# Norming the tokens once 1/rms is known, and emptying the projection banks on ScalarE

## Chip, core and metric

One kernel runs on one core of a Trainium2 chip. The metric is the device time of one execution in microseconds. Each comparison uses the median of several runs.

## What is computed

The kernel is one decoder layer for 512 tokens of width 1024. Cut to what matters here:

```
u    = x * rsqrt(mean(x*x) + eps) * g                 # RMSNorm of the tokens, 512 x 1024
proj = u @ w_in                                       # 1024 x 5888
qa, ka, va, qb, kb, vb, qm, gl = split(proj)          # three attentions' inputs, three gates
y0, y1, y2 = window(qa, ka, va), stick_breaking(qb, kb, vb), memory(qm, mem)
merged = sum_b sigmoid(gl_b) * (y_b @ w_branch_b)
h   = x + rms_norm(merged @ w_out)
out = h + rms_norm(swiglu_ffn(rms_norm(h)))
```

## The kernel before

**Number format.** Every large matmul is done as three: each fp32 operand is split into a high part, which ScalarE (ACT) rounds by a copy, and a low part, which VectorE (DVE) gets by a subtraction (`split`, L132 to L139). `mm3` (L164) multiplies high by high, high by low and low by high into one PSUM bank.

**Layout.** The tokens lie transposed: eight tiles of 128 features x 512 tokens (`xraw`, loaded from `xT`). `u[k]` holds the two parts of tile k. Before the change these parts are of x times the gain `g_pre`, not yet divided by the rms, because 1/rms needs the whole of x first: its squares are summed (L540 to L543, in place in `xraw`), summed over the features by a matmul with ones (`ss_x`), and turned into `rb` by `rstd_of` and `rsqrt` (L209 to L228). `rb` holds 1/rms of every token, the same in all 128 partitions. A bank of products is therefore multiplied by `rb` when it is emptied (`evac` in `proj`, L289 to L297, on DVE). For the values, whose bank has tokens on the partitions, `per_token` (L230) turns `rb` with four PE transposes into one number per token, `rs`, and `val` (L325) scales with it.

**The stream.** `Stream` holds the weight units in their order; one unit is 512 KB or less, loaded, split and multiplied. `dn.run(us)` emits so many microseconds of pieces (a piece is three to a few matmuls, by a duration written beside it); `dn.until(flag)` emits all up to a flag; loads are emitted four units and splits three units ahead. The order of the units is: four key units of the stick-breaking attention (`kb`), four query units (`qb`), six units of values in two halves (`val`, banks `pv`), then `ka`, two `qa`, the memory's keys and values, two more `qa`, and for each branch eight gate units (`g`), with four `qm` units and the branch products between. A unit of `proj` is 24 matmuls of 512 columns, `val` has 96 matmuls of 320 columns in each half.

**Banks and tiles.** Two PSUM banks (`dps`) serve `proj` (the `kb` units use four of the six `aps` banks, since they have to wait for `rb`); `val` uses four `aps` banks in each half. Nearly all tiles of 512 columns come from one pool of 68, `ck`.

**Order of the work.** The first part, to the unloading of the four `kb` banks, is in `tc.manual_schedule()`: there each engine issues in the order of the code. After it the tile framework orders each engine's instructions when the program is built, by their place in the code and by readiness; `tc.high_priority()` puts an instruction ahead of others that are ready. On the chip each engine keeps that order. After `evac`, `kb` and `qa` are split into stacked halves by `stack_parts` (L254), `qb` and `ka` by `stack_twice` (L265).

Of the kernel before, what the change touches and what calls it, by code (L numbers as in the profile page):

```python
# [13 lines left out]
AF = mybir.ActivationFunctionType  # L14
ALU = mybir.AluOpType
# [4 lines left out]
S = 512  # L20
M = 256
KC = D // P
# [81 lines left out]
def tile_kernel(ctx, tc, a):  # L104
    nc = tc.nc
# [12 lines left out]
    def ck(name, dt=F32):  # L118
        return ckp.tile([P, 512], dt, tag="ck", name=name)
# [10 lines left out]
    st = {}  # L130

    def split(raw, hi, lo):  # L132

        ins = nc.scalar.copy(hi, raw)  # L134
        lows = nc.vector.tensor_tensor(lo, raw, hi.bitcast(F32), op=ALU.subtract)  # L135
        if "behind" in st:
            after(ins, st["behind"][0])
            after(lows, st["behind"][1])
        return ins  # L139
# [22 lines left out]
    dn = Stream(w_load, w_split)  # L162

    def mm3(out, l, r, start, stop):  # L164
        (lh, ll), (rh, rl) = l, r
        nc.tensor.matmul(out, lh, rh, start=start, stop=False, skip_group_check=True)  # L166
        nc.tensor.matmul(out, lh, rl, start=False, stop=False, skip_group_check=True)  # L167
        nc.tensor.matmul(out, ll, rh, start=False, stop=stop, skip_group_check=True)  # L168
# [4 lines left out]
    def cols(hl, o, n):  # L173
        return hl[0][:, o : o + n], hl[1][:, o : o + n]
# [3 lines left out]
    def after(ins, first):  # L178
        dep = mybir.DependencyInfo(mybir.DependencyClass.NoSync, mybir.DependencyReason.DATA)
        tc.add_manual_dep(ins.ins, first.ins.name, dep, reason="order")  # L180

    def fn(*args, **kw):

        ins = nc.scalar.activation(*args, **kw)  # L184
        for p in pin:
            after(ins, p)
        since.append(ins)
        return ins
# [41 lines left out]
    def per_token(name, rb, n, bank):  # L230

        pt = bank(f"st_{name}")
        for t in range(n // P):
            nc.tensor.transpose(pt[:, t * P : (t + 1) * P], rb[:, t * P : (t + 1) * P], ident[:, :])
        rs = cst.tile([P, n // P], F32, name=f"rs_{name}")
        nc.vector.tensor_copy(rs[:, :], pt[:, :n].rearrange("p (t n) -> p t n", n=P)[:, :, 0])
        return rs
# [9 lines left out]
    u = [None] * KC  # L247

    def parts(name, t):
        h, l = ck(f"{name}h", F32R), ck(f"{name}l", F32R)  # L250
        split(t[:, :], h[:, :], l[:, :])
        return h, l

    def stack_parts(kind, idx, t):  # L254

        for e in range(2):
            r, o = 64 * e, 64 - 64 * e
            x = ck(f"{kind}s{idx}{e}", F32R)
            nc.scalar.copy(x[r : r + 64, :], t[r : r + 64, :])
            nc.vector.tensor_tensor(  # L260
                x[o : o + 64, :], t[r : r + 64, :], x[r : r + 64, :].bitcast(F32), op=ALU.subtract
            )
            st[(kind + "s", idx, e)] = x

    def stack_twice(kind, idx, t):  # L265

        for e in range(2):
            r, o = 64 * e, 64 - 64 * e
            x = ck(f"{kind}s{idx}{e}", F32R)
            lo = ck(f"{kind}l{idx}{e}", F32R)  # L270
            nc.gpsimd.memset(lo[o : o + 64, :].bitcast(F32), 0.0)
            st[(kind + "l", idx, e)] = lo
            nc.scalar.copy(x[r : r + 64, :], t[r : r + 64, :])
            nc.vector.tensor_tensor(
                lo[r : r + 64, :], t[r : r + 64, :], x[r : r + 64, :].bitcast(F32), op=ALU.subtract
            )
            nc.vector.tensor_copy(x[o : o + 64, :], t[r : r + 64, :])
            st[(kind + "s", idx, e)] = x

    def proj(kind, idx):  # L280
        def gen(hi, lo):
            ps = (aps if kind == "kb" else dps)(f"{kind}{idx}")
            for k in range(KC):
                mm3(ps[:, :], cols((hi, lo), k * P, P), u[k], k == 0, k == KC - 1)
                yield 0.65
            t = ck(f"{kind}{idx}")
            s = 0.125 if kind in ("qa", "qb") else 1.0

            def evac():  # L289
                with tc.high_priority():  # L290
                    nc.vector.scalar_tensor_tensor(t[:, :], ps[:, :], s, st["rb"][:, :], op0=ALU.mult, op1=ALU.mult)  # L291
                if kind in ("kb", "qa"):
                    stack_parts(kind, idx, t)
                elif kind in ("qb", "ka"):
                    stack_twice(kind, idx, t)
                elif kind == "qm":
                    st[("qms", idx)] = parts(f"qms{idx}", t)  # L297

            if "rb" in st:
                evac()  # L300
            else:
                st.setdefault("waiting", []).append(evac)
            st[(kind, idx)] = t

        return gen

    def gate(b, c):
        def gen(hi, lo):
            yield from proj(f"g{b}", c)(hi, lo)
            g = st[(f"g{b}", c)]  # L310

            if b in st.get("sigmoid", ()):
                dn.later(2.0, lambda: fn(g[:, :], g[:, :], AF.Sigmoid))

        return gen

# [8 lines left out]
    def val(h, q):  # L325
        def gen(hi, lo):
            if q == 0:
                st["pv"] = [aps(f"pv{h}{t}") for t in range(NT)]
            for i in range(3 if q < 2 else 2):
                k = 3 * q + i  # L330
                for t in range(NT):
                    x = (u[k][0][:, t * P : (t + 1) * P], u[k][1][:, t * P : (t + 1) * P])
                    mm3(st["pv"][t][:, :320], x, cols((hi, lo), i * 320, 320), k == 0, k == KC - 1)
                    yield 0.41
                    if k == KC - 1:
                        nc.vector.tensor_scalar(
                            v_all[:, t * 640 + h * 320 : t * 640 + (h + 1) * 320],
                            st["pv"][t][:, :320],
                            st["rs"][:, t : t + 1],
                            None,  # L340
                            op0=ALU.mult,
                        )

        return gen

    v_all = cst.tile([P, NT * 640], F32, name="v_all")
# [92 lines left out]

    for c in range(8):  # L440
        dn.add(a["w_p"][:, c].rearrange("p k n -> p (k n)"), 1024, proj("kb" if c < 4 else "qb", c % 4))
    for h in range(2):
        for q in range(3):
            n = 3 if q < 2 else 2
            dn.add(a["w_v"][:, h, 3 * q : 3 * q + n].rearrange("p k n -> p (k n)"), n * 320, val(h, q))
# [29 lines left out]
    xraw = []  # L475
# [28 lines left out]
    with tc.manual_schedule():  # L504

        idle = cst.tile([P, 512], BF16, name="idle")
        nc.vector.memset(idle[:, :], 0.0)
        pw = dps("warm")
        for i in range(WARM):
            mm(pw[:, :], idle[:, :P], idle[:, :], True, True)  # L510

        first_load(nc.scalar, 0)
        first_table = nc.scalar.preload_act_table_set("natural_log_exp_and_others")
        g_pre = const("g_pre", [P, KC])
        load_x(0, 3)
        first_load(nc.sync, 1)
        load_x(3, 5)
        first_load(nc.sync, 2)
        load_x(5, 8)
        dn.loaded = dn.have = FIRST  # L520
        first_split(0, 0)
        gain_split(0)
        for i in range(1, FIRST):
            first_split(i, 0)
        gain_split(1)
        gain_split(2)
        for p in (1, 2):
            for i in range(FIRST):
                first_split(i, p)
            for k in range(*PIECE[p]):  # L530
                if u[k] is None:
                    gain_split(k)
        dn.ahead(4, 3)
        gens = [dn.units[i]["mm"](his[i], los[i]) for i in range(FIRST)]
        for k in range(KC + 1):
            for g in gens:
                next(g, None)
        dn.at = FIRST
        xacc = ck("xacc")
        nc.scalar.activation(xacc[:, :], xraw[0][:, :], AF.Square)  # L540
        for k in range(1, KC):
            nc.scalar.activation(xraw[k][:, :], xraw[k][:, :], AF.Square)
            nc.vector.tensor_tensor(xacc[:, :], xacc[:, :], xraw[k][:, :], op=ALU.add)  # L543
        while dn.at < 4:
            dn.piece()
        st["rb"] = rstd_of("x", xacc, S, aps)
        for f in st.pop("waiting"):
            f()
# [16 lines left out]
    none_r = cst.tile([P, P], F32R, name="none_r")  # L565
    nc.gpsimd.tensor_copy(none_r[:, :], none[:, :])

    st["rs"] = per_token("x", st["rb"], S, aps)
    dn.until("sb_ready")


# [519 lines left out]
    rb = {}  # L1091
# [317 lines left out]
```

## Time and profile before

| what | value |
|---|---|
| median of three runs | 813.15 us (813.1 to 813.63) |
| profiled execution | 813.76 us, span 812.0 us |
| TensorE (PE) busy | 800.4 us, 99% of the span, 4727 matmuls |
| DVE busy | 589.7 us, 73% |
| ACT busy | 440.0 us, 54% |
| POOL busy | 85.0 us, 10% |
| share of PE in the chain that ended last | 92% |

Engines: PE multiplies, PEld loads its weights beside it, DVE is VectorE, ACT is ScalarE, POOL is GpSimd, SP issues most DMAs. A row of the timeline has the start in us, the duration in us, the engine, the line of the kernel, the operation, output<-inputs, the shapes and the count; in brackets stands the idle time before it and what ended it. A matmul's duration is longer than the distance to the next one, since matmuls overlap; the distance is what PE needs for one. A row of waits has who waited for whom, the total in us, how many times and the longest.

### The profile page before, as it was taken

The numbers are of one execution on the slowest core, as the hardware profiler recorded it, in microseconds if no ns is written. First come the engines' busy times: TensorE is split into PE (matmuls) and PEld (weight loads), VectorE is DVE, ScalarE is ACT, GpSimd is POOL, SyncE is SP. The second block draws the span as 40 slices with busy tenths as digits, with TensorE's granted clock in tenths as the row PEclk, the third lists the DMA queues.
The fourth block names the chain that finished last, engine by engine and source line by source line (L and its number), as shares of the span: only waits on it lengthen the run. The fifth ranks groups of instructions, "written<-read, shape, count | busy, mean of one in ns | idle before, by whom it ended". The sixth has DMA issues, their size and how long they took to land.

```text
span 812.0 us, 12349 instructions
## 1 busy us (share of the span) xinstructions
PE 800.4 (99%) x4727; PEld 702.8 (87%) x4727; DVE 589.7 (73%) x939; ACT 440.0 (54%) x787; POOL 85.0 (10%) x103
## 2 busy tenths in 40 slices
PE   9999999999999999999999999999999999999996
PEld 6789888778888888888888899999999999988885
DVE  5886779656488843773384869977676777898797
ACT  6554667556655533552362566655555555666573
POOL 3003200000000000221004200110000000205200
PEclk9999999999999999999999999999999999999998
DMA  8334534321221223213359936887767662759902
GB/s 270 121 113 142 184 103 132 93 61 53 78 79 52 79 82 99 79 52 100 86 163 377 246 66 167 248 209 186 194 177 191 176 172 88 177 131 224 207 1 104
DMA packets 37741, 112.94 MB, mean 139 GB/s; under 512 B 4625, under 2 KB 6177, under 8 KB 37681
## 3 DMA queue, kind: packets, MB, share of 16 engines
q1 hardware_dynamic: 29232, 86.07, 33.2%
q0 software_dynamic: 8016, 25.68, 16.5%
q8 instruction: 37, 0.61, 0.3%
q10 hardware_dynamic: 432, 0.39, 0.2%
q14 instruction: 24, 0.19, 0.1%
HBM read 108.46 MB, written 3.67 MB: 138 GB/s over the span
## 4 chain that ended last, share of the span: by engine, by line
PE 92%; DVE 3%; DMA 2%; ACT 1%; issue 1%; SPq 0%; ACTq 0%; DVEq 0%
PE g L166 5%; PE g L167 5%; PE g L168 5%; PE gx L166 5%; PE gx L168 5%; PE gx L167 5%; PE z L171 4%; PE br L166 3%; PE br L167 3%; PE br L168 3%; PE gy L168 3%; PE gy L166 3%; PE gy L167 3%; PE x L168 2%; PE x L167 2%; PE x L166 2%
## 5 line engine op out<-in xcount | busy, mean ns | idle before, releaser
L134 ACT CAST hi<-raw 128x1024 fp32r<-128x1024 f32 (+2 forms) x64 | 65.8, 1035 | 109.7 <-issue 51.8
L134 ACT CAST hi<-gw 128x1024 fp32r<-128x1024 f32 x77 | 79.8, 1048 | 82.3 <-DVE gw L994 40.1
L135 DVE TENSOR_TENSOR lo<-gw,hi 128x1024 fp32r<-128x1024 f32 x77 | 93.5, 1223 | 33.6 <-ACT hi L134 33.6
L135 DVE TENSOR_TENSOR lo<-raw,hi 128x1024 fp32r<-128x1024 f32 (+2 forms) x64 | 78.2, 1226 | 17.6 <-ACT hi L134 17.5
L166 PE MATMUL g<-uh,hi 128*128 128x512 f32 x192 | 75.6, 394 | 0.0
L168 PE MATMUL g<-uh,lo 128*128 128x512 f32 x192 | 74.8, 389 | 0.0
L167 PE MATMUL g<-ul,hi 128*128 128x512 f32 x192 | 74.8, 389 | 0.0
L291 DVE SCALAR_TENSOR_TENSOR g<-g,rb_x 128x512 f32<-128x512 f32 x24 | 16.4, 689 | 54.7 <-PE g L168 54.5
L976 POOL DMA_DIRECT2D gw<-in_w_gu x27 | 23.4, 906 | 187.4 <-DMA gw<-in_w_gu 61.2
L168 PEld LDWEIGHTS g<-uh,lo 128*128 128x128 f32 x192 | 36.0, 188 | 7.6
L166 PEld LDWEIGHTS g<-uh,hi 128*128 128x128 f32 x192 | 36.1, 188 | 7.5 <-issue 0.3
L167 PEld LDWEIGHTS g<-ul,hi 128*128 128x128 f32 x192 | 36.1, 188 | 7.1
L134 ACT CAST hi<-r 128x1024 fp32r<-128x1024 f32 (+1 forms) x24 | 23.6, 982 | 19.9 <-PE y L168 5.3
L167 PE MATMUL x<-lo,lh 128*128 128x512 f32 x88 | 34.2, 389 | 0.0
L166 PE MATMUL x<-hi,lh 128*128 128x512 f32 x88 | 34.2, 389 | 0.0
L168 PE MATMUL x<-hi,ll 128*128 128x512 f32 x88 | 34.1, 389 | 0.0
L135 DVE TENSOR_TENSOR lo<-r,hi 128x1024 fp32r<-128x1024 f32 (+1 forms) x24 | 27.1, 1131 | 3.7 <-ACT hi L134 3.6
L184 ACT ACTIVATE e<-e 128x384 f32<-128x384 f32 (+1 forms) x48 | 26.9, 561 | 1.5
L134 ACT CAST hi<-bp 128x512 fp32r<-128x512 f32 x33 | 19.1, 620 | 13.4 <-PE y L168 4.8
L641 DVE SCALAR_TENSOR_TENSOR e<-z,e 128x384 f32<-128x384 f32 (+1 forms) x24 | 14.3, 598 | 15.9 <-ACT e L184 15.9
L166 PE MATMUL gx<-T4h,hi 128*128 128x256 f32 x88 | 25.1, 285 | 0.4 <-ACT hi L134 0.4
L166 PE MATMUL gy<-N22h,hi 128*128 128x256 f32 x88 | 25.1, 285 | 0.2 <-ACT hi L134 0.2
(539 smaller groups left out, 2614.0 us busy)
## 6 DMA issues: line engine op xcount, KB each, us to landing
gw<-in_w_gu SPq DMA_DIRECT2D x57, 512.0 KB, 4.9
raw<-in_w_p SPq DMA_DIRECT2D x38, 512.0 KB, 3.5
gw<-in_w_gu POOLq DMA_DIRECT2D x27, 512.0 KB, 7.7
raw<-in_w_br SPq DMA_DIRECT2D x12, 512.0 KB, 3.6
bp<-in_w_dn SPq DMA_DIRECT2D x22, 256.0 KB, 8.1
r<-in_w_dn POOLq DMA_DIRECT2D x10, 512.0 KB, 8.2
raw<-in_w_out SPq DMA_DIRECT2D x8, 512.0 KB, 3.6
bp<-in_w_dn POOLq DMA_DIRECT2D x11, 256.0 KB, 12.6
```

Source lines behind the costliest of these rows:

```text
L134: ins = nc.scalar.copy(hi, raw)
L135: lows = nc.vector.tensor_tensor(lo, raw, hi.bitcast(F32), op=ALU.subtract)
L166: nc.tensor.matmul(out, lh, rh, start=start, stop=False, skip_group_check=True)
L167: nc.tensor.matmul(out, lh, rl, start=False, stop=False, skip_group_check=True)
L168: nc.tensor.matmul(out, ll, rh, start=False, stop=stop, skip_group_check=True)
L171: return nc.tensor.matmul(out, l, r, start=start, stop=stop, skip_group_check=True)
L184: ins = nc.scalar.activation(*args, **kw)
L291: nc.vector.scalar_tensor_tensor(t[:, :], ps[:, :], s, st["rb"][:, :], op0=ALU.mult, op1=ALU.mult)
L641: nc.vector.scalar_tensor_tensor(x, z[i][:, :n], 0.0, x, op0=ALU.max, op1=ALU.add)
L976: nc.gpsimd.dma_start(gw[(n, key)][:, :], g_src(n, i, j), accum_op=ALU.add)
```

## The change

The tokens are normed once `rb` is there: `normed(k)` multiplies `xraw[k]` in place by the gain and `rb` on DVE and splits it anew (ACT copy, DVE subtraction) into two tiles. After each of the eight, 2.5 us of the stream are emitted. After the `qb` units (flag `plain`) `u` holds the new parts, and `st["whole"]` is set. All units from the values on read these. Their banks need no scale: `proj` empties them by an ACT multiplication with a constant, or, for a gate whose branch's sigmoids have already been applied, by the sigmoid itself, which `gate` applied later before. `val` empties its banks by plain copies at high priority, even tiles on ACT and odd ones on DVE. `per_token` is no longer called for x. The squares go to tiles of their own, since `xraw` is still needed.

```diff
+            whole = "whole" in st
             def evac():
                 with tc.high_priority():
-                    nc.vector.scalar_tensor_tensor(t[:, :], ps[:, :], s, st["rb"][:, :], op0=ALU.mult, op1=ALU.mult)
+                    if not whole:
+                        nc.vector.scalar_tensor_tensor(t[:, :], ps[:, :], s, st["rb"][:, :], op0=ALU.mult, op1=ALU.mult)
+                    elif kind[0] == "g" and int(kind[1]) in st.get("sigmoid", ()):
+                        fn(t[:, :], ps[:, :], AF.Sigmoid)
+                    else:
+                        nc.scalar.mul(t[:, :], ps[:, :], s)
...
     def gate(b, c):
         def gen(hi, lo):
             yield from proj(f"g{b}", c)(hi, lo)
-            g = st[(f"g{b}", c)]
-            if b in st.get("sigmoid", ()):
-                dn.later(2.0, lambda: fn(g[:, :], g[:, :], AF.Sigmoid))
...
                     if k == KC - 1:
-                        nc.vector.tensor_scalar(
-                            v_all[:, t * 640 + h * 320 : t * 640 + (h + 1) * 320],
-                            st["pv"][t][:, :320],
-                            st["rs"][:, t : t + 1],
-                            None,
-                            op0=ALU.mult,
-                        )
+                        with tc.high_priority():
+                            vt = v_all[:, t * 640 + h * 320 : t * 640 + (h + 1) * 320]
+                            if t % 2 == 0:
+                                nc.scalar.copy(vt, st["pv"][t][:, :320])
+                            else:
+                                nc.vector.tensor_copy(vt, st["pv"][t][:, :320])
...
         dn.add(a["w_p"][:, c].rearrange("p k n -> p (k n)"), 1024, proj("kb" if c < 4 else "qb", c % 4))
+    dn.mark("plain")
...
-            nc.scalar.activation(xraw[k][:, :], xraw[k][:, :], AF.Square)
-            nc.vector.tensor_tensor(xacc[:, :], xacc[:, :], xraw[k][:, :], op=ALU.add)
+            xs = ck(f"xs{k}")
+            nc.scalar.activation(xs[:, :], xraw[k][:, :], AF.Square)
+            nc.vector.tensor_tensor(xacc[:, :], xacc[:, :], xs[:, :], op=ALU.add)
...
-    st["rs"] = per_token("x", st["rb"], S, aps)
+    def normed(k):
+        x = xraw[k]
+        nc.vector.scalar_tensor_tensor(
+            x[:, :], x[:, :], g_pre[:, k : k + 1], st["rb"][:, :], op0=ALU.mult, op1=ALU.mult
+        )
+        return tuple(t[:, :] for t in parts(f"n{k}", x))
+
+    un = []
+    for k in range(KC):
+        un.append(normed(k))
+        dn.run(2.5)
+    dn.until("plain")
+    u[:] = un
+    st["whole"] = True
     dn.until("sb_ready")
```

## The prediction

> **What bounds the kernel now.** I read the page's shares and chain first, then who made TensorE (PE) wait, then the order of PE's and VectorE's (DVE's) instructions around the places where it waited, then busy time by stage.
>
> ```profile
> span 812.0 us, 12349 instructions
> PE 800.4 (99%) x4727; PEld 702.8 (87%) x4727; DVE 589.7 (73%) x939; ACT 440.0 (54%) x787; POOL 85.0 (10%) x103
> PEclk9999999999999999999999999999999999999998
> PE 92%; DVE 3%; DMA 2%; ACT 1%; issue 1%; SPq 0%; ACTq 0%; DVEq 0%
> ```
> ```profile
> PE warm L171 <- DVE idle L507: 1.3, 1, 1.3
> PE st_x L234 <- DVE rb_x L216: 0.9, 1, 0.9
> PE pv L166 <- DVE v_all L336: 0.9, 1, 0.9
> PE gx L166 <- ACT hi L134: 0.4, 1, 0.4
> PE qb L166 <- DVE qb L291: 0.4, 1, 0.4
> ...
> ```
>
> PE is busy for 800.4 of 812.0 us and is 92% of the chain that ended last. So work taken from DVE or given to ScalarE (ACT) is worth nothing by itself; it counts only where PE waits. The list of PE's waits (total, times, longest; three more are 0.3 or less) is short. The change can touch three of them: `st_x`, `qb` and `pv`. The next view is PE's order around these three.
>
> ```profile
> 32.86 0.39 PE L167 MATMUL qb<-ul,hi 128*128 128x512 f32 x1
> 33.09 0.39 PE L168 MATMUL qb<-uh,lo 128*128 128x512 f32 x1
> 34.42 0.66 PE L234 MATMUL st_x<-c_ident,rb_x 128*128 128x128 f32 x4 [0.94 <-DVE rb_x L216]
> 34.83 0.47 PE L166 MATMUL qb<-uh,hi 128*128 128x512 f32 x1
> ...
> 41.76 0.30 PE L166 MATMUL pv<-hi,uh 128*128 128x320 f32 x1
> ...
> 44.83 0.31 PE L166 MATMUL pv<-hi,uh 128*128 128x320 f32 x1
> 45.55 0.50 PE L166 MATMUL qb<-uh,hi 128*128 128x512 f32 x1 [0.41 <-DVE qb L291]
> ...
> 69.34 0.41 PE L166 MATMUL pv<-hi,uh 128*128 128x320 f32 x1 [0.87 <-DVE v_all L336]
> ```
>
> Matmuls of 512 columns start 0.23 us apart (32.86, 33.09), those of 320 columns 0.147 (22 of them from 41.76 to 44.83). Three losses are seen. From 33.32 to 34.83, 1.51 us, PE waits for 1/rms and transposes it. From 44.98 to 45.55, 0.57 us, the third query unit (qb2) waits for a bank. At 69.34 the value matmuls wait 0.87 us. Together they are 2.95 us, and this is all that the change can win. One more thing counts: between 41.76 and 44.98 PE had no bank for qb2 and did 22 value matmuls (3.2 us) instead. DVE, in the same stretch, shows why the bank was late:
>
> ```profile
> 33.67 0.69 DVE L216 SCALAR_TENSOR_TENSOR rb_x<-t_x,rb_x 128x512 f32<-128x512 f32 x1
> 34.40 0.69 DVE L291 SCALAR_TENSOR_TENSOR kb<-kb,rb_x 128x512 f32<-128x512 f32 x1
> 35.77 1.39 DVE L260 TENSOR_TENSOR kbs<-kb,kbs 64x512 fp32r<-64x512 f32 x2 [0.50 <-ACT kbs L259]
> ...
> 37.78 1.15 DVE L135 TENSOR_TENSOR lo<-raw,hi 128x960 fp32r<-128x960 f32 x1
> ...
> 41.74 1.39 DVE L260 TENSOR_TENSOR kbs<-kb,kbs 64x512 fp32r<-64x512 f32 x2 [0.69 <-ACT kbs L259]
> 43.14 0.69 DVE L291 SCALAR_TENSOR_TENSOR kb<-kb,rb_x 128x512 f32<-128x512 f32 x1
> 43.75 1.15 DVE L135 TENSOR_TENSOR lo<-raw,hi 128x960 fp32r<-128x960 f32 x1
> 44.81 0.68 DVE L291 SCALAR_TENSOR_TENSOR qb<-qb,rb_x 128x512 f32<-128x512 f32 x1
> ```
>
> The bank of qb0 was full soon after 36 (six matmuls after 34.83), but DVE emptied it at 44.81, behind all four key units (kb0 to kb3: 0.69 to unload, 1.39 to split). It did so although it idled for 0.69 before 41.74 and ran two weight splits in gaps. So the unload of qb0 does not slip into the key chain, high priority or not. My reading, not shown, is that its tile gets a slot of the shared pool only after those of earlier instructions.
>
> ```profile
> 34.40:45.50 11.10, 10.72 (x56) 9.25 (x56) 9.77 (x14) 6.96 (x10) 0.00 (x0) 1.00 0.16 44
> 45.50:56.60 11.10, 11.05 (x49) 9.14 (x50) 10.01 (x17) 4.50 (x8) 0.00 (x0) 1.00 0.36 101
> 56.60:69.30 12.70, 11.87 (x81) 11.60 (x79) 11.31 (x18) 9.31 (x17) 3.75 (x4) 1.00 0.54 173
> ```
>
> Columns after the stretch's length: PE, PEld, DVE, ACT. From 34.4 to 69.3 DVE is busy 31.1 of 34.9 us: 3.8 us are free, just where the change adds work.
>
> **The change part by part.** Prices of the added work:
>
> ```profile
> L291 DVE SCALAR_TENSOR_TENSOR g<-g,rb_x x24: 677/692/692, 172.6 to 407.9; 128x512 f32<-128x512 f32 x24
> L184 ACT ACTIVATE g<-g x24: 612/624/630, 208.7 to 409.2; 128x512 f32<-128x512 f32 x24
> L134 ACT CAST mgh<-g x8: 612/621/624, 412.7 to 431.6; 128x512 fp32r<-128x512 f32 x8
> L135 DVE TENSOR_TENSOR mgl<-g,mgh x8: 681/684/687, 414.4 to 433.9; 128x512 fp32r<-128x512 f32 x8
> L336 DVE TENSOR_SCALAR v_all<-pv,rs_x x8: 536/541/546, 68.7 to 82.9; 128x320 f32<-128x320 f32 x8
> ```
>
> (1) Norming: eight times a DVE scale (0.69), an ACT copy (0.62) and a DVE subtraction (0.68). That is 11.0 us on DVE and 5.0 on ACT, where DVE has 3.8 us free.
>
> (2) The four transposes and the copy to `rs_x` go: PE runs on from 33.32 instead of 34.83, a gain of 1.51.
>
> (3) The squares go to tiles of their own: same instructions, nothing. No DMA and no POOL instruction is added or moved on its queue. The shared pool of 68 tiles holds, while both sets of token parts live, 16 old, 16 new, at most 8 raw, 8 key parts, 16 query parts and 4 unsplit queries; each normed tile frees its raw one, so it stays below 68, with little to spare. A shortage would hold the last norming until the queries are done: case E.
>
> (4) ACT unloads all 33 later banks (24 gates, 1 ka, 4 qa, 4 qm) at about 0.62 instead of DVE at 0.69; the late gates of the last branch need one ACT instruction where there was a DVE and an ACT one. PE waits nowhere in those stages and one unit's 24 matmuls take 5.5 us for an unload of 0.62, so zero; if ACT's queue is in the way for longer than the other bank's unit lasts, that excess is paid. I keep 0 to 2 us for it.
>
> (5) Value banks: four of eight unloads go to ACT, all at high priority. The wait of 0.87 goes, since one unload (0.54) is shorter than the two tiles that PE still has banks for (six matmuls, 0.9 us).
>
> (6) The value units now read the normed tokens. So they cannot stand in while qb2 waits: the stand-in of 41.76 to 44.98 is gone unless the first normed token tile is ready.
>
> The stall follows. PE ends qb1 at 41.76 - 1.51 = 40.2. DVE has 1/rms at 34.36. The key chain is 4 x 0.69 + 4 x 1.39 = 8.3 us. Its four gaps, where it waits for ACT, now hold ready work: three scales (2.1) and a weight split (1.15). With the unload of qb0 (0.69) this ends at 34.36 + 8.3 + 3.2 + 0.7 = 46.6. If the subtractions of the first three tiles come first (the code's order, if slots are given in that order), it ends at 48.7, but then the first normed tile is there at about 46.6 and value matmuls stand in from then. Both ways PE idles from 40.2 to 46.6, 6.4 us. From below: with gaps unfilled and free, 43.4, a stall of 3.2; from above: 48.7 without a stand-in, 8.5. I take 6.4, which both orders give. Later, PE has 11 us of queries and 14 us of first-half values (96 x 0.147), to 71.7; DVE still has, after 46.6, three unloads (2.1), four query stacks (8.9, each two 0.69 and two 0.42 beside row L274/L277), the rest of the norming (8.9) and two splits (2): 21.9 us, to 68.5, so it is just in time.
>
> ```profile
> L274 DVE TENSOR_TENSOR qbl<-qb,qbs x8: 674/686/689, 47.5 to 59.1; 64x512 fp32r<-64x512 f32 x8
> L277 DVE CAST qbs<-qb x8: 421/422/424, 48.2 to 57.9; 64x512 fp32r<-64x512 f32 x8
> ```
>
> Stall 6.4 less the three losses 2.95: +3.45 us.
>
> (7) A second price of the stall is PE's speed after it. The program's start shows it:
>
> ```profile
> 1.35 4.43 PE L171 MATMUL warm<-idle 128*128 128x512 bf16 x11 [1.35 <-DVE idle L507]
> 1.75 0.15 PEld L171 LDWEIGHTS <-idle 128*128 128x128 bf16 x1 [0.28 <-issue]
> 2.18 0.15 PEld L171 LDWEIGHTS <-idle 128*128 128x128 bf16 x1 [0.28 <-issue]
> ```
>
> After the idle start, 512-column matmuls come 0.43 us apart, against 0.23 later, though the clock row reads full. Eleven of them lose 11 x 0.20 = 2.2 us. No later idle in this trace is over 1.3 us, so it does not tell whether 6.4 us brings the slow rate back. From below 0, from above 2.2, a whole new start. I take 2.2, since the only long idle that the trace has was followed by it.
>
> The Trainium skill, "TensorE: Matmul & The Clock Gate", section "HAM oscillation", says that PE idle for more than about 3.4 us falls back to half clock, for about 3.4 us of work. By that rule the term would be 1.7, an estimate, and the time 818.3; the start above (4.4 us at half rate) fits it, and no stall here tests it.
>
> Sum: the profiled execution took 813.76 us (its span is 812.0), 0.6 above the median of 813.15. It gains 2.95 and loses 6.4 and 2.2: 819.4, or **818.8** on the median.
>
> **Rivals.**
> B, the stall comes but PE keeps its rate: +3.45, 816.6. For it: nothing in the trace slows after the short waits. Against: they are short.
>
> C, a short stall: DVE's gaps stay unfilled and the unload ends at 43.4 to 44.5; stall 3.2 to 4.3, +0.3 to +1.4, so 813.4 to 814.6. Against it: two splits were put into such gaps before.
>
> D, faster: DVE unloads qb0 before PE ends qb1 at 40.2, in the gap at 35.1 or 37.8. Then PE never stops for qb2; queries end at 51.2, the last normed tile is due 12.3 us later at 63.5, and DVE's work to there, with three stacks ahead of it, is 32 us from 34.36, to 66.3; with the stacks after it, 59.7. So between -2.95 and 0; at -1.5 it is 811.6. Against it: the same gaps passed qb0 by in this trace. It decides at 40.2.
>
> E, worse: the stall as forecast, and norming also late for the value units, or ACT late with later banks: +2 to +4 more, 821 to 823.
>
> That the relief of DVE pays nothing after 83 us is in all of them.
>
> **How the numbers follow.** This kernel's three runs spread 0.07%; 0.2% (1.6 us) is about what can be told. Chances: forecast 0.38, B 0.22, C 0.16, D 0.15, E 0.09. The forecast, B and E are slower (0.69), C is the same but for its upper edge (0.15 and 0.01), D is faster about four times in five (0.12 and 0.03). Slower 0.70, same 0.18, faster 0.12. The range 812.6 to 822 leaves out D and part of E; the forecast's own range is 817 to 820.5.
>
> **What would show it.** In the changed profile: no `st_x`; the wait of PE for `qb` grows from 0.4 to over 5 us and ends on DVE L291's successor or a normed tile; DVE nearly without idle from 34 to 69; `pv` no longer waits near 69; after the stall, PE's matmuls 0.43 apart for some us; PE's waits after 83 us as short as now. The prediction is wrong if DVE unloads qb0 before 40.2, if the queries' order is another, or if PE finds other ready work in the stall.

## The result: 8.8 us slower, and the profile after

| | before | after |
|---|---|---|
| median of the compared runs | 813.36 us (813.1 to 813.63) | 822.19 us (821.67 to 822.56) |
| ratio after to before | | 1.0102, interval [1.009, 1.0114] |
| profiled execution / span | 813.76 / 812.0 us | 821.67 / 819.5 us |

The forecast was 818.8, slower with a chance of 0.70. The direction held. The time lay above the forecast's own range (817 to 820.5) and just above the upper end of the whole range (822.0); the ratio, applied to the 813.15 that the forecast started from, gives 821.4.

The page of the changed kernel: span, busy time, and the clock row in 40 slices of 20.5 us.

```profile
span 819.5 us, 12347 instructions
PE 801.7 (98%) x4723; PEld 704.1 (86%) x4723; DVE 575.9 (70%) x917; ACT 459.2 (56%) x824; POOL 84.9 (10%) x103
PEclk9989999999999999999999999999999999999998
```

DVE lost 14 us of work and ACT gained 19; PE's own work hardly changed. Who made PE wait (total, times, longest):

```profile
PE pv L166 <- ACT n0h L134: 7.6, 1, 7.6
...
PE pv L166 <- DVE v_all L344: 0.7, 1, 0.7
...
PE pv L166 <- ACT v_all L342: 0.4, 1, 0.4
```

There is one new wait of 7.6 us, for the high part of the first normed tile. `st_x` and `qb` are gone from the list, and `v_all` waits twice instead of once. PE's order around these places:

```profile
39.54 0.39 PE L168 MATMUL qb<-uh,lo 128*128 128x512 f32 x1
47.48 0.64 PE L166 MATMUL pv<-hi,n0h 128*128 128x320 f32 x1 [7.56 <-ACT n0h L134]
...
50.54 0.43 PE L167 MATMUL pv<-lo,n0h 128*128 128x320 f32 x1
50.80 0.31 PE L168 MATMUL pv<-hi,n0l 128*128 128x320 f32 x1
...
52.12 0.39 PE L166 MATMUL qb<-uh,hi 128*128 128x512 f32 x1
...
75.57 0.41 PE L166 MATMUL pv<-hi,n0h 128*128 128x320 f32 x1 [0.36 <-ACT v_all L342]
76.97 0.41 PE L166 MATMUL pv<-hi,n0h 128*128 128x320 f32 x1 [0.70 <-DVE v_all L344]
```

The last matmul of qb1 starts at 39.54 and takes its 0.23 us, so PE stands from 39.77 to 47.48, 7.71 us. From 47.48 to 50.80 it does 11 value matmuls in 3.32 us; at 0.147 each they would need 1.62, so 1.70 us are lost to the slow rate. Then the spacing is 0.147 again, and qb2 starts at 52.12. DVE and ACT show why so late:

```profile
33.27 0.69 DVE L216 SCALAR_TENSOR_TENSOR rb_x<-t_x,rb_x 128x512 f32<-128x512 f32 x1
...
34.60 1.41 DVE L575 SCALAR_TENSOR_TENSOR xT<-xT,c_g_pre,rb_x 128x512 f32<-128x512 f32 x2
38.08 0.74 DVE L575 SCALAR_TENSOR_TENSOR xT<-xT,c_g_pre,rb_x 128x512 f32<-128x512 f32 x1
38.74 1.15 DVE L135 TENSOR_TENSOR lo<-raw,hi 128x960 fp32r<-128x960 f32 x1
...
41.93 1.40 DVE L575 SCALAR_TENSOR_TENSOR xT<-xT,c_g_pre,rb_x 128x512 f32<-128x512 f32 x2
...
45.41 1.15 DVE L135 TENSOR_TENSOR lo<-raw,hi 128x960 fp32r<-128x960 f32 x1
...
48.03 0.69 DVE L135 TENSOR_TENSOR n0l<-xT,n0h 128x512 fp32r<-128x512 f32 x1
48.64 0.75 DVE L575 SCALAR_TENSOR_TENSOR xT<-xT,c_g_pre,rb_x 128x512 f32<-128x512 f32 x1
...
50.56 0.68 DVE L135 TENSOR_TENSOR n2l<-xT,n2h 128x512 fp32r<-128x512 f32 x1
51.17 0.68 DVE L294 SCALAR_TENSOR_TENSOR qb<-qb,rb_x 128x512 f32<-128x512 f32 x1
```
```profile
45.53 1.26 ACT L259 CAST kbs<-kb 64x512 fp32r<-64x512 f32 x2 [2.22 <-DVE kb L294]
46.81 0.62 ACT L134 CAST n0h<-xT 128x512 fp32r<-128x512 f32 x1
```

The first normed tile was scaled at 34.60, but ACT copies it only at 46.81, right behind the copies of the last key unit, although ACT had idled for 2.22 us before those. That copy ends at 47.43 and lets PE go on. DVE unloads the bank of qb0 at 51.17, behind the whole key chain (to 48.0, with five scales and two weight splits in its gaps), three low parts and two more scales. The windows of both stretches (length, PE, PEld, DVE, ACT, POOL, granted clock, DMA share, GB/s):

```profile
34.40:45.50 11.10, 5.53 (x25) 4.25 (x23) 10.85 (x17) 5.71 (x8) 1.04 (x2) 0.93 0.16 45
45.50:56.60 11.10, 9.12 (x40) 8.10 (x41) 10.94 (x17) 5.28 (x9) 0.00 (x0) 0.76 0.15 44
```

DVE is full (10.85 and 10.94 of 11.1), PE is not, and the second stretch's clock is 0.76.

**A ruler for the rest.** Between profiled executions `rb` comes at 32.77 to 34.35 us whatever the kernel, so whole spans compare badly. Two stretches are steadier: from the start of `rb` (33.67 before, 33.27 after) to `pbias`, the first matmul behind the values, and from `pbias` to the last matmul. Their rows in the kernel before and in the changed one:

```profile
82.75 0.91 PE L171 MATMUL pbias<-oh,rb 32*128 32x384 f32 x2
804.68 0.39 PE L168 MATMUL x<-hi,ll 128*128 128x512 f32 x1
```
```profile
89.93 0.91 PE L171 MATMUL pbias<-oh,rb 32*128 32x384 f32 x2
812.12 0.39 PE L168 MATMUL x<-hi,ll 128*128 128x512 f32 x1
```

Worked out so for all profiles, with the compared ratios:

| kernel | rb to pbias | pbias to last matmul | ratio to before, interval |
|---|---|---|---|
| before | 49.08 | 721.93 | 1 |
| after | 56.66 | 722.19 | 1.0102 [1.009, 1.0114] |
| after_again (the changed kernel once more) | 56.67 | 722.23 | 1.0106 [1.0092, 1.0119] |
| a_queries_first | 61.60 | 722.20 | 1.0136 [1.0118, 1.0154] |
| a_fill | 56.45 | 722.21 | 1.0091 [1.0078, 1.0105] |
| a_dve_unload | 56.66 | 721.95 | 1.0088 [1.0074, 1.0102] |
| a_own | 49.61 | 722.22 | 1.0014 [1.0005, 1.0023] |
| a_own_act | 48.16 | 723.70 | 0.9999 [0.999, 1.0008] |
| b_norm_unused | 50.98 | 721.97 | 1.0022 [1.0013, 1.0031] |
| b_own | 47.97 | 721.93 | 0.9988 [0.998, 0.9996] |
| b_own_late | 49.54 | 721.94 | 0.9999 [0.999, 1.0009] |
| b_own_late_pri | 48.04 | 721.94 | 0.9999 [0.999, 1.0008] |
| b_best | 47.91 | 721.94 | 0.9993 [0.9984, 1.0002] |

The change costs 7.58 us before `pbias` and 0.26 behind it, 7.84 together. The rows of PE in this profile add up to nearly the same: 7.71 of standing, 1.70 of slow rate, 1.06 of new waits for `v_all` and 0.26 at the back, less the 2.95 that went away, are 7.78. What remains to the 8.8 of the medians are the scatter of the start and 0.41 outside the span (821.67 - 819.5 = 2.17, before 1.76), whose cause isn't settled.

### The profile page after: what moved, and what is told of

The parts are those of the page before. It is cut to its first block, busy times and chain, and to the rows that moved or that the text cites. A ratio compares the mean times of both kernels' runs of the same rounds, so it can differ in the third digit from the quotient of the medians.

```text
span 819.5 us, 12347 instructions
## 1 busy us (share of the span) xinstructions
PE 801.7 (98%) x4723; PEld 704.1 (86%) x4723; DVE 575.9 (70%) x917; ACT 459.2 (56%) x824; POOL 84.9 (10%) x103
## 4 chain that ended last, share of the span: by engine, by line
PE 93%; DVE 5%; ACT 1%; issue 1%; DVEq 0%; ACTq 0%
PE g L166 5%; PE g L168 5%; PE g L167 5%; PE gx L166 5%; PE gx L168 5%; PE gx L167 5%; PE z L171 4%; PE br L166 3%; PE br L168 3%; PE br L167 3%; PE gy L168 3%; PE gy L166 3%; PE gy L167 3%; PE x L168 2%; PE x L167 2%; PE x L166 2%
## 5 line engine op out<-in xcount | busy, mean ns | idle before, releaser
L134 ACT CAST hi<-gw 128x1024 fp32r<-128x1024 f32 x77 | 79.8, 1048 | 82.3 <-DVE gw L1012 40.2
L135 DVE TENSOR_TENSOR lo<-bp,hi 128x512 fp32r<-128x512 f32 x33 | 22.3, 708 | 5.8 <-ACT hi L134 5.5
L166 PE MATMUL gx<-B11h,hi 128*128 128x256 f32 x88 | 25.1, 285 | 0.2 <-ACT B11h L923 0.2
L166 PE MATMUL mx<-woh,mgh 128*128 128x512 f32 x64 | 25.0, 391 | 0.0
L168 PE MATMUL gw<-B21h,lo 128*128 128x256 f32 x88 | 25.0, 284 | 0.0
L168 PE MATMUL gy<-N22h,lo 128*128 128x256 f32 x88 | 25.0, 284 | 0.0
L167 PE MATMUL gx<-B11l,hi 128*128 128x256 f32 x88 | 25.0, 284 | 0.0
L168 PE MATMUL mx<-woh,mgl 128*128 128x512 f32 x64 | 24.9, 389 | 0.0
```

## The experiments

Kernels a_ start from the changed kernel, b_ from the kernel before. The theory: the stall is made by the order in which slots of the shared pool are given (the raw tile of qb0 stands behind earlier code), together with the loss of the stand-in. The rivals: the half rate after the stall, ACT's later unloads, or DVE's overload as such.

**a_fill: keep PE warm through the stall.** 32 matmuls of zeros that nobody reads, behind qb1.

```diff
+        if k == 4:
+            pf = aps("fill")
+            for i in range(32):
+                ins = mm(pf[:, :], idle[:, :P], idle[:, :], True, True)
+                after(ins, st["last_qb1"])
```

> The changed kernel with 32 extra matmuls of zeros (512 columns, 0.23 us each, 7.3 us in all) on TensorE right behind the second query unit, where it idles from 39.77 to 47.48 us. Their results are not used; nothing else is changed. Theory (the stall costs twice, the idle itself and a slow restart): the idle is now filled, the value matmuls after it are 0.147 us apart instead of 0.27, and the time falls by the slow restart alone, 12 matmuls x 0.125 us = 1.5 to 1.7 us, to 820.5. Rival (the 0.27 us spacing has another cause, such as waiting for the normed parts): no change, 822.2.

Measured: 821.59 us, between the theory's 820.5 and the rival's 822.2. PE's waits and the window:

```profile
PE pv L166 <- DVE v_all L346: 0.9, 1, 0.9
PE pv L168 <- DVE n0l L135: 0.7, 1, 0.7
PE qb L166 <- DVE qb L296: 0.5, 1, 0.5
...
```
```profile
45.50:56.60 11.10, 9.54 (x47) 7.14 (x46) 10.94 (x17) 5.29 (x9) 0.00 (x0) 1.00 0.16 46
```

The clock is back from 0.76 to 1.00, so the slow rate came from the stall. But the time hardly moved: PE, faster now, waits 0.7 for a low part and 0.5 for the bank of qb0, both from DVE, and 0.3 for the first normed tile. From `rb` to `pbias` it saves 0.21 us of the 1.70 lost in the rows. The slow restart ran beside DVE's late unload.

**a_dve_unload: the later banks emptied by DVE again**, unscaled. (The gates whose bank is emptied by the sigmoid kept that on ACT, other than the expectation says.)

```diff
-                        nc.scalar.mul(t[:, :], ps[:, :], s)
+                        nc.vector.tensor_scalar(t[:, :], ps[:, :], s, None, op0=ALU.mult)
```

> The changed kernel with the 33 later projection banks emptied by VectorE again, by a multiplication with a constant, and the sigmoids of the last branch's late gates fused no longer but left out there (so those gates stay without their sigmoid; the time is what is asked). The value banks stay as changed. Theory (nothing after 83 us waits for these unloads): 822.2 within 0.5 us. Rival (ScalarE's queue delays banks in the later stages and part of the 8.8 us is lost there): faster by 1 us or more.

Measured: 821.25 us, below the expected 821.7 to 822.7. Its two rows:

```profile
89.97 0.91 PE L171 MATMUL pbias<-oh,rb 32*128 32x384 f32 x2
811.92 0.39 PE L168 MATMUL x<-hi,ll 128*128 128x512 f32 x1
```

The back part takes 721.95 us, as before the change; with ACT it takes 722.19. All five profiles with ACT's unloading and no slow stretch there have 722.19 to 722.23, the seven without it 721.93 to 721.97. So the 0.26 behind `pbias` is ACT's unloading; of the 33 banks 25 went back to DVE here. The front keeps its loss. By the medians the gain is larger, 0.94 us; 0.38 of it lies outside the span (2.17 in the changed kernel, 821.09 - 819.3 = 1.79 here), and a_own, with ACT's unloading, has 1.76 there, so this part isn't explained by it.

**a_own: tiles of their own for the four unscaled queries**, instead of slots of the shared pool.

```diff
+    qown = [cst.tile([P, 512], F32, name=f"qown{i}") for i in range(4)]
...
-            t = ck(f"{kind}{idx}")
+            t = qown[idx] if kind == "qb" else ck(f"{kind}{idx}")
```

> The changed kernel with four tiles of their own for the unscaled queries qb, instead of slots of the shared pool; the work is the same. Theory (the unload of qb0 is held until earlier instructions have their slots, so TensorE finds no bank): VectorE unloads qb0 in the first gap, about 35.5 us, TensorE runs through all four query units to about 50.7, the idle of 7.7 us and the slow restart go, and what is left is up to 2 us where the last normed tile is late: 811 to 814. Rival (VectorE simply has 11 us too much work in this stretch, in whatever order): TensorE waits as long, but for the normed tiles, after the queries: 819 or more.

Measured: 815.06 us (814.22 to 815.97), above the expected 811 to 814. DVE's unload of qb0, and PE's waits that are left:

```profile
35.92 0.69 DVE L296 SCALAR_TENSOR_TENSOR qown<-qb,rb_x 128x512 f32<-128x512 f32 x1
```
```profile
PE pv L169 <- DVE lo L137: 1.6, 1, 1.6
...
PE pv L170 <- DVE n7l L137: 0.5, 1, 0.5
...
PE pv L170 <- DVE n5l L137: 0.4, 1, 0.4
```

No instruction changed, only where a tile lives: the unload moved from 51.17 to 35.92, the stall went, and rb to `pbias` fell by 7.05 us. So the shared pool's slot is what held the unload and made the stall. That the slots are given in the code's order is the reading; that the pool of 68 was short of free ones would have the same cure, and a_queries_first below speaks for the order. The norming still overloads DVE: three waits of 2.5 us together stand where the 2.95 were won.

**b_norm_unused: the kernel before, with the eight normings added and nobody reading them.**

```diff
+    for k in range(KC):
+        normed(k)
+        dn.run(2.5)
+    dn.until("plain")
```

> The kernel before with the eight normings added at the same place (and the squares in tiles of their own), but with nobody reading them: values, gates and all else read the old parts and scale as before. Theory (the norming's 11 us on VectorE hurt only because the value matmuls can no longer stand in while the third query unit has no bank): qb0 is unloaded at about 51 as in the changed kernel, but value matmuls fill the time; 813.4 to 815. Rival (the load on VectorE alone makes it slow): 819 or more.

Measured: 815.58 us, just above the expected 813.4 to 815 and far from the rival's 819. DVE's unload and PE's waits:

```profile
50.92 0.69 DVE L291 SCALAR_TENSOR_TENSOR qb<-qb,rb_x 128x512 f32<-128x512 f32 x1
```
```profile
PE pv L166 <- DVE v_all L336: 1.3, 1, 1.3
PE pv L167 <- DVE lo L135: 1.2, 2, 0.9
```

The unload is as late as in the changed kernel (50.92 against 51.17), yet the price up to `pbias` is 1.90 us in place of 7.58: values that read the old parts stand in. A late bank alone makes no stall; a late bank without other work for PE does.

**after_again and a_queries_first.** The changed kernel once more, beside a version whose normings are emitted behind the queries:

```diff
-    un = []
-    for k in range(KC):
-        un.append(normed(k))
-        dn.run(2.5)
     dn.until("plain")
-    u[:] = un
+    u[:] = [normed(k) for k in range(KC)]
```

> The changed kernel itself, as the measure for the filled and the reordered kernels on one chip. Expected 822.2 within 0.5 us if the clock's slow restart costs what the filled kernel seemed to save (0.6 us against the other call); 821.5 if that was a difference between calls only.

> The changed kernel with all eight normings emitted behind the four query units instead of between their pieces; same instructions. Theory (slots of the pool are given in the code's order): the unload of qb0 then waits for the key chain alone and comes at about 47.5 us instead of 51.2, but the normed tiles come only behind the query stacks, at about 63, so TensorE idles twice, 7.7 us before the third query unit and 3 us before the values: 823 to 825. Rival (the normings between the pieces are what delays TensorE, and queries first is the remedy): 816 to 818.

Measured: after_again 822.24 us, 1.0106 [1.0092, 1.0119], so by the medians a_fill and a_dve_unload gain 0.65 and 0.99 us over it. Its profile is a second one of the same program, and the slow restart is longer in it: PE stands for 8.26 us, then does 16 matmuls at the slow rate (48.23 to 52.89) and loses 2.3 us by it in place of 1.70, and waits for `v_all` only once, 0.70. Yet `rb` to `pbias` takes 56.67 us, against 56.66. So PE's losses in this stretch stand in for one another, and the sum of PE's rows above is one way of booking them.

a_queries_first 824.16 us (823.1 to 827.15), 1.0136 [1.0118, 1.0154], as forecast; the waits in its profile (of its longest execution):

```profile
PE qb L166 <- ACT kbs L259: 7.6, 1, 7.6
PE pv L166 <- ACT n0h L134: 2.7, 1, 2.7
```

DVE unloads qb0 from 47.37 to 48.05, 12.4 us behind the end of `rb` in place of 17.2, with the order of the code alone changed. (The first row names ACT's last key copy, which ends at 48.09.) The first stall is as long as before, though no low part of a normed tile stands ahead of qb0's unload any more: the query comes sooner, but now no values stand in at all. A second stall of 2.7 follows for the norming. Moving the normings in the code trades one wait for another; it doesn't take the unload out of the key chain.

**a_own_act: a_own, with the queries' cross-half copies (L277) on ACT**, to relieve DVE.

```diff
-            nc.vector.tensor_copy(x[o : o + 64, :], t[r : r + 64, :])
+            nc.scalar.copy(x[o : o + 64, :], t[r : r + 64, :])
```

> The changed kernel with own tiles for the unscaled queries, and the eight (later also two) copies across halves in the query and key split moved from VectorE (0.42 us each) to ScalarE. Theory (with the order mended, only VectorE's 11 us too much are left, seen as three waits of TensorE of 0.4, 0.5 and 1.6 us): VectorE loses 3.4 us of work ahead of these waits, they shrink to under 0.7 us together, and the time is 1 to 2.5 us below that of the kernel with own tiles alone, 0.9970 to 0.9995 of before. Rival (ScalarE's queue becomes the one that is late): no gain against own tiles alone, 1.001 or more of before.

Measured: 813.75 us (812.47 to 815.07). That is 1.3 below a_own, within the 1 to 2.5 expected; the ratio, 0.9999, is just above its expected range. The front part is 1.45 us shorter than a_own's. But in this profile (the slowest execution, 815.07) the back part is 1.5 longer:

```profile
82.25 0.91 PE L173 MATMUL pbias<-oh,rb 32*128 32x384 f32 x2 [1.14 <-POOL rb L601]
...
85.48 0.63 PE L169 MATMUL ka<-n0l,hi 128*128 128x512 f32 x1
85.91 0.63 PE L170 MATMUL ka<-n0h,lo 128*128 128x512 f32 x1
```

Behind a wait of 1.14 us the matmuls come 0.43 apart until about 87.9. In the kernel before, no slow rate was seen behind waits of 0.9 us.

**b_best, b_own, b_own_late, b_own_late_pri: what the other parts are worth without norming.** b_own is the kernel before with the own tiles of a_own. b_own_late also emits the transposes of 1/rms behind the queries:

```diff
+    dn.until("plain")
     st["rs"] = per_token("x", st["rb"], S, aps)
```

b_own_late_pri also empties the value banks at high priority (DVE); b_best does that with the even ones on ACT.

> The kernel before, without norming, with three edits that take its three losses of 2.95 us one by one: own tiles for the unscaled queries (0.57), the transposes of 1/rms emitted behind the query units (the wait of 1.1; the transposes' 0.41 stays), and the value banks emptied at high priority, even ones by ScalarE with the per-token scale (0.87). Theory (these waits are all that the change could win): 2.0 to 2.5 us faster than before, 0.9970 to 0.9978. Rival (TensorE waits elsewhere instead, as VectorE is as full as ever): within 0.5 us of before.

> The kernel before with tiles of their own for the four unscaled queries, and nothing else changed. The theory (the pool's slots are given in the order of the code, so that qb0's unload stands behind the key chain): qb0 is unloaded near 36 to 38 us instead of 44.81, PE no longer waits for qb (0.41 and the 0.16 around it go), and the value matmuls no longer have to stand in; the transposes (1.5) and the wait for v_all (0.9) stay. So 0.3 to 0.7 us faster than before, ratio 0.9990 to 0.9997, hardly to be told from it; and the changed kernel with such tiles (1.0014) is then 1.2 to 1.8 us slower than this one, which is the price of the change itself. Rival (the unload's place comes from DVE's load, not from the slots): qb0 is unloaded after 42 us and nothing changes.

> The kernel before with own tiles for the four unscaled queries, and the four transposes of 1/rms emitted behind the queries. Theory: PE runs from qb0 through the queries without waiting for 1/rms, 1.2 us (the wait of 0.94 and the queue around it; the four transposes still cost about 0.3) and the 0.57 at qb2 go; the wait for v_all near 69 stays. 1.3 to 2.0 us faster than before, ratio 0.9975 to 0.9984. Rival: PE, early by that much, waits the same time at the next late buffer (a weight part or v_all), and the ratio is 0.9992 to 1.0000, as it was with the values' banks shared with ACT.

> As the run before this (own tiles, late transposes), and the values' banks emptied at high priority, all eight by DVE. Theory: of the waits of PE for v_all (0.9 before, 1.5 where ACT emptied half of these banks) 0.5 or less is left, since DVE does not have to wait for ACT's queue; 0.4 to 0.9 us faster than the run before this, ratio to the kernel before 0.9965 to 0.9978. Rival: the wait for v_all moves or grows, since DVE is busy with the queries' halves there, and it equals the run before this within 0.4 us.

Measured: b_own 812.29 us (811.83 to 815.48), b_best 812.68 (811.87 to 815.57), b_own_late_pri 813.12 (812.29 to 814.92), b_own_late 813.88 (812.04 to 815.33). Only b_own's interval stays below 1. In b_own, DVE's unload of qb0, PE's waits and its `pbias`:

```profile
36.88 0.68 DVE L293 SCALAR_TENSOR_TENSOR qown<-qb,rb_x 128x512 f32<-128x512 f32 x1
```
```profile
PE pv L168 <- DVE v_all L338: 0.5, 1, 0.5
...
PE st_x L236 <- DVE rb_x L218: 0.2, 1, 0.2
```

The unload moved from 44.81 to 36.88 and the wait for `qb` is gone, as the theory had it; the interval of the size (1.0 us, 0.3 to 1.6) takes in what was expected (0.3 to 0.7). The late transposes then give nothing that can be told: PE waits for `v_all` instead, 1.5 us in b_best (even banks on ACT), 1.6 in b_own_late_pri, 2.3 in b_own_late. None of the three reached its theory, and by the ratios their rivals hold (b_best's 0.6 us is just over the 0.5 named). In b_own_late a slow stretch follows that wait:

```profile
68.95 0.41 PE L168 MATMUL pv<-hi,uh 128*128 128x320 f32 x1 [2.29 <-DVE v_all L338]
...
70.95 0.47 PE L170 MATMUL pv<-hi,ul 128*128 128x320 f32 x1
71.22 0.47 PE L168 MATMUL pv<-hi,uh 128*128 128x320 f32 x1
```

So the fastest version that I found, though not told apart from b_best, is the kernel before with four tiles of its own for the unscaled queries. With the same tiles the change itself costs 2 to 3 us: by the ratios 1.0014 against 0.9988, by the medians 815.06 against 812.29, by the two stretches 1.64 + 0.29.

## Why the prediction was right in kind and short in size

Right, with its rows or runs:

- The place and the mechanism. PE stopped behind qb1, for a normed tile, because qb0's bank was emptied behind the key chain and the values could no longer stand in. The reading on slots, "not shown" then, is shown by a_own and b_own (one edit of where a tile lives moved the unload by 15 us in the one and, counted from `rb`, by 7 in the other; a_queries_first supports the order), and the lost stand-in by b_norm_unused.
- Term (2): no `st_x`, no wait for 1/rms. Term (3): no loss is seen from the squares' own tiles.
- Term (4): put at zero, it is 0.26 us behind `pbias` (a_dve_unload).
- Norming just in time for the first half of the values: the list of PE's waits of the changed kernel has none for `n1` to `n7`. It was in time because the stall had delayed PE; without the stall (a_own) PE waits for `n5l` and `n7l`.

Wrong:

- **The stall, 6.4.** It was 7.71. Counted from the end of `rb`, PE stopped at 5.81 us (the prediction: 5.84) and restarted at 13.52 (12.24). The step that failed is the filling of the key chain's gaps: "three scales (2.1) and a weight split (1.15)" were five scales and two splits. That put the last key unit's unload on DVE at 44.80, and ACT's copy of the first normed tile, which ends the stall, behind the copies of that unit at 45.53. Then two more scales stood between the low parts, so qb0 was unloaded at 51.17, not at 48.0. Whether tiles of their own for the normed parts would let ACT copy the first one in its earlier gaps was not tried.
- **Term (7), 2.2 for a slow restart.** The restart was slow, and its rows lose 1.70. But taking it away (a_fill) gives back 0.21 between `rb` and `pbias`, and 0.6 by the medians, since DVE unloads qb0 only at 51.17 and PE would have waited there instead. The term took a loss in PE's rows for a price without asking what ends next.
- **Term (5), a wait of 0.87 gone.** It became 0.36 + 0.70 = 1.06 (0.70 in after_again's profile). High priority did not bring DVE's unload ahead of the two parts of the memory (`ml`) that it did first:

```profile
74.85 1.66 DVE L242 SCALAR_TENSOR_TENSOR ml<-mT,c_g_mem,mh 128x256 fp32r<-128x256 f32 x2 [0.37 <-ACT mh L241]
76.44 0.88 DVE L344 COPY v_all<-pv 128x320 f32<-128x320 f32 x2
```

In the prediction's own sum, 6.4 + 2.2 - 2.95 = 5.65, the rows put 7.71 for 6.4 (+1.31), 1.70 for 2.2 (-0.50), 1.06 of new `v_all` waits (+1.06) and 0.26 for the later banks (+0.26): 7.78. The slow rate's 1.70 counts there as a loss of PE's rows; with PE at full rate (a_fill) most of it came back as waits for DVE.

Of the rivals, C (a short stall, gaps unfilled) and D (qb0 emptied before 40.2) fell with the row at 51.17. D's order is what a_own forces (unload at 35.92), and there D's own doubt was borne out: the last normed tiles came late, and instead of 811.6 it took 815.06. B was, in effect, near the truth on the slow rate: PE lost the rate but the kernel hardly paid. E named the right total (821 to 823) for another reason.

## What to carry to other kernels

When a list of waits shows an engine emptying a bank late although it idled before, look for what its output tile waits for: in these runs a slot of the shared pool came by the order of the code, and a tile of its own can move the instruction by many microseconds, for the space of the tile. Before you move work ahead of a critical chain, look for the work that stands in while the chain is late; if the change makes that work depend on the chain, the hidden delay becomes a stall. And price a slow stretch only after asking which other engine sets the next deadline.

## What the hardware showed that I had not expected

- PE's half rate comes in stretches of a fixed length. Narrow windows of the granted clock show it at 0.50 from 43.96 to 50.78 in the changed kernel (6.83 us), 42.63 to 52.87 in after_again (10.24), 45.29 to 52.12 in a_dve_unload (6.83), 43.57 to 53.81 and 64.05 to 70.88 in a_queries_first (10.24 and 6.83), 70.33 to 73.74 in b_own_late and 84.46 to 87.88 in a_own_act (3.41 each): one, two or three times 3.41 us. Three rows, all within such stretches, in the changed kernel, after_again and b_own_late:

```profile
44.00:50.70 6.70, 3.22 (x11) 2.96 (x12) 6.54 (x11) 2.90 (x5) 0.52 (x1) 0.50 0.24 73
42.70:52.80 10.10, 4.57 (x16) 4.31 (x17) 9.91 (x16) 4.30 (x8) 0.52 (x1) 0.50 0.24 80
70.40:73.70 3.30, 3.30 (x14) 3.30 (x14) 1.00 (x1) 0.00 (x0) 0.00 (x0) 0.50 0.63 194
```

- In these seven the clock falls 2.2 to 5.4 us after PE has stopped, whether PE has resumed or not. Behind the stalls of 7.6 to 8.3 us, and behind 2.9 us of standing in a_queries_first, the slow rate is there when PE resumes; behind the waits of 2.29 (b_own_late) and 1.14 us (a_own_act) it comes 1.4 and 2.2 us later. Waits of 1.6 (a_own, b_own_late_pri) and 1.5 us (b_best) show none in their profiles. The Trainium skill, "TensorE: Matmul & The Clock Gate", section "HAM oscillation", has half clock after more than about 3.4 us of idle: the stalls of 7.6 to 8.3 us agree; the 2.9, 2.29 and 1.14 us do not, and here the measurement decides. In the 3.41 us ahead of the fall PE had been busy for at most 1.38 us, but for 2.27 in a_own_act, so what amount of work keeps the clock up was not settled.
- The profiles of b_own_late and a_own_act are of long executions (814.99 in 812.04 to 815.33, and 815.07 in 812.47 to 815.07), those of a_own, b_best and b_own_late_pri of short ones. So a program may meet the slow stretch in some executions and not in others; one profile of each does not show it.
- The granted clock shows these stretches (0.76 in the window behind the stall), though it showed none at the program's start, where the same spacing of 0.43 stood beside a full clock row.
- The moment of `rb` scatters from 32.77 to 34.35 us between profiled executions; one and the same program, the changed kernel, has it at 33.27 and at 34.01. It is a scatter of a size with what most of these edits are worth, which is why a stretch between two events told them apart where the spans did not.
